# A two-layer block with adaLN: part of the adaLN pieces, and c, loaded by Pool's queue instead of SyncE's

## The chip, the cores and the metric

The kernel runs on one core of one Trainium2 chip. The metric is the time of one execution on the device, in microseconds (us). The core has five engines that work side by side, each through its own instructions in their order: TensorE (PE: matmuls; PEld: its weight loads), VectorE (DVE), ScalarE (ACT), GpSimd (POOL) and SyncE (SP). SP computes nothing here; its queue issues transfers between memory and the chip. ACT's and POOL's queues can issue transfers too. An instruction that waits for a semaphore holds up everything behind it on its own engine. All transfers are carried by the core's 16 DMA engines.

## The reference

Two layers over one sequence of 256 rows of 2048 features, all in float32. A vector c of 2048 numbers gives, by a large matrix per layer, six rows of 2048: shift, scale and gate for the mixer, and the same for the feed-forward (adaLN).

```python
c_act = jax.nn.silu(c)
for i in range(DEPTH):                       # 2 layers
    ada = c_act @ ada_w[i] + ada_b[i]        # ada_w[i]: 2048 x 12288
    shift1, scale1, gate1, shift2, scale2, gate2 = jnp.split(ada[:, None, :], 6, axis=-1)
    h = rms_norm(x, norm1_g[i]) * (1.0 + scale1) + shift1
    m = diff_attention(h, ...) if i == 0 else mamba2_ssd(h, ...)
    x = x + gate1 * m
    h = rms_norm(x, norm2_g[i]) * (1.0 + scale2) + shift2
    x = x + gate2 * swiglu(h, ffn_w_gate_up[i], ffn_w_down[i])   # hidden 5632
```

Layer 0 mixes by differential attention, layer 1 by a Mamba-2 block (SSD): a projection to 4096 gates z, 6144 channels that pass a short convolution, and 64 step sizes; a chunked scan over two chunks of 128 rows; and a projection from 4096 back to 2048.

## The kernel before

**Stages.** The work runs through attention, the first feed-forward, the SSD block and the second feed-forward, one after another. Every weight matrix is read once, in units of 256 rows by 512 columns, 512 KB each. A unit is loaded by SP into one of seven raw buffers (L284, `split_unit`). ACT copies it to its high part `wh` in a reduced format (L288), DVE subtracts to get the low part `wl` (L290; the profile shows every DVE and PE operation under L137, the helper that issues them), and TensorE multiplies twelve times: two row blocks, two k tiles, and the products high by high, low by high, high by low. Up to four units stand ready ahead of TensorE.

**Order.** The order is written by the program itself. Units go through a list; when one is taken out and multiplied, `tick` runs: it gives each open chain of small steps (a Python generator in `active`) one step (`step_all`), and, at a rate set per stage, takes adaLN jobs from the list `jobs`.

**adaLN.** The adaLN products are spread under the other work as pieces of 512 KB, each loaded into one of the same seven raw buffers and consumed by DVE one tick later. There are two kinds. For shift and scale, `col_jobs` (L506) loads 128 output features by half of c's length (L514), and DVE multiplies by c, which stands in all partitions as the two tiles `cB`, and sums along the row (`raw<-raw,cB` in the profile). For a gate, `ada_job` (L461) loads 128 rows of the matrix by 1024 columns (L474; the bias at L472) and DVE adds it, times an entry of c, to the tile `acc` (`acc<-raw,cT,acc`). When a half of 1024 columns is complete, `fin_gate` (L526) has Pool sum `acc` over the 128 partitions, 512 columns at a time, into the gate row (L532), two all-reduces per half.

The stages take the following jobs. At the first feed-forward's entry, `jobs0` (L1469) queues shift and scale of layer 1's mixer and 16 of the pieces for its feed-forward, and stores c to memory (L1478), as the room of `cB` is taken by `acc` later. While its down products run, gate 2 of layer 0 is made (`down`, L1405, 34 pieces). At the SSD block's entry, `later_jobs` (L1491) fetches c again (L1494) and queues the 48 pieces left over, then gate 1 of layer 1 (34 pieces); the rate stays 0 until the scan begins (L1787). The second feed-forward makes its own gate (34 pieces).

**What else is on the queues.** SP also loads the scan's decay tables (L1664), one per group of heads. ACT issues the DMA transposes of the feed-forward's activations (L1372). Pool computes the reciprocal roots of the norms (`rstd_of`, L448 and L449), issues a few small loads and the stores of the output, and fills constants at the SSD block's entry (L1510 to L1513).

Of the kernel before, what the change touches and what calls it, by code (L numbers as in the profile page):

```python
# [35 lines left out]
ADA_UNITS = 156  # L36
# [77 lines left out]
def block_kernel(ctx: ExitStack, tc: tile.TileContext, x, c, positions, norm1_g, norm2_g, ada_w, ada_b,  # L114
# [8 lines left out]
    pe, act, dve, pool, sp = nc.tensor, nc.scalar, nc.vector, nc.gpsimd, nc.sync  # L123
# [47 lines left out]
    def bcast(ap1, n):  # L171
        return bass.AP(tensor=ap1.tensor, offset=ap1.offset, ap=[[0, 128], [1, n]])
# [7 lines left out]
    limit = {"u": W_BUFS}  # L180
    jobs = deque()
    ripe = deque()
    ada = {"rate": 0.0, "acc": 0.0}
    free = {"wk": 3, "po": 1, "epi": EPI, "e0": 3, "e1": 1, "on": 1}

    def take(what, n=1):
# [10 lines left out]
    def start(gen):  # L197
        if next(gen, StopIteration) is not StopIteration:
            active.append(gen)
        return gen  # L200
# [77 lines left out]
    def call(fn):  # L278
        fifo.append(("c", fn))
# [121 lines left out]
    class Columns:  # L401
# [12 lines left out]
        def finish(self, i):  # L414
            t = self.groups[i][0]
            n = t.shape[1]
            ps = bank("wk")
            pe.transpose(ps[:, :n], self.st[:n, i, :], ident[:n, :n])
            dve.tensor_copy(t, ps[:, :n])
# [39 lines left out]
    mods = {}  # L459

    def ada_job(layer, vec, finish, gate=False):  # L461
        st = {}
        last = 16 if gate else 15

        def unit(hf, k):
            def run():
                col = vec * D + hf * 1024
                raw = rawp.tile([128, 2, 512], F32, tag="raw", name="raw")
                rv = raw.rearrange("p a n -> p (a n)")
                load["dma"] += 1270.0  # L470
                if k == 16:
                    sp.dma_start(rv, bcast(ada_b[layer, col:col + 1024], 1024))  # L472
                else:
                    sp.dma_start(rv, ada_w[layer, k * 128:(k + 1) * 128, col:col + 1024])  # L474

                def use():
                    if k == 0:
                        st["acc"] = rowp.tile([128, 1024], F32, tag="acc", name="acc", bufs=2)
                        dve.tensor_scalar(st["acc"], rv, cT[:, 0:1], None, op0=ALU.mult)
                    else:  # L480
                        acc = st["acc"]
                        dve.scalar_tensor_tensor(acc, rv, 1.0 / 128.0 if k == 16 else cT[:, k:k + 1], acc,
                                                 op0=ALU.mult, op1=ALU.add)
                    if k == last:
                        acc = st["acc"]
                        ripe.append([1, lambda: finish(acc, hf)])
                ripe.append([RIPE, use])
            return run
        for hf in range(2):
            for k in range(last + 1):  # L490
                jobs.append(unit(hf, k))

    cB = []

    def col_item(layer, vec, kt, hf):
        at = (((4 * layer + (0, 1, 3, 4).index(vec)) * 16 + kt) * 2 + hf) * 131072
        return bass.AP(tensor=ada_t.tensor, offset=ada_t.offset + at, ap=[[1024, 128], [1, 1024]])

    def col_sum(st, rv, layer, vec, kt, hf, t):

        if hf == 0:
            st[kt] = small(1, "half")
        dve.tensor_tensor_reduce(rv, rv, cB[hf], 1.0, st[kt] if hf else b_cols[layer, vec][:, kt:kt + 1],
                                 ALU.mult, ALU.add, t[:, kt:kt + 1] if hf else st[kt])

    def col_jobs(layer, vec, key, g=None):  # L506
        t = mods["T" if g is None else "S", key] = const.tile([128, 16], F32, name=f"col{vec}{key}")
        st = {}

        def unit(kt, hf):  # L510
            def run():
                rv = rawp.tile([128, 2, 512], F32, tag="raw", name="raw").rearrange("p a n -> p (a n)")
                load["dma"] += 1270.0
                sp.dma_start(rv, col_item(layer, vec, kt, hf))  # L514

                def use():
                    col_sum(st, rv, layer, vec, kt, hf, t)
                    if g is not None and (kt, hf) == (15, 1):
                        dve.scalar_tensor_tensor(t, t, 1.0, g, op0=ALU.add, op1=ALU.mult)
                ripe.append([RIPE, use])  # L520
            return run
        for kt in range(16):
            for hf in range(2):
                jobs.append(unit(kt, hf))

    def fin_gate(key):  # L526
        def f(acc, hf):
            if hf == 0:
                mods["G", key] = rowp.tile([128, D], F32, tag="gate", name="gate")
            for i in range(2):  # L530
                o = hf * 1024 + i * 512
                pool.partition_all_reduce(mods["G", key][:, o:o + 512], acc[:, i * 512:(i + 1) * 512], 128,  # L532
                                          ReduceOp.add)
        return f


# [365 lines left out]
    gate = {"next": 0, "raws": []}  # L902
# [434 lines left out]
    def ffn(layer, end, first_jobs, final):  # L1337
        key = f"f{layer}"
# [5 lines left out]
        def enter():  # L1344
            end["leave"]()
            if layer == 0:
                ssd_consts()
            st["low"] = low.enter_context(tc.tile_pool(name=f"low{layer}", bufs=1))
            st["top"] = top.enter_context(tc.tile_pool(name=f"top{layer}", bufs=1))
            first_jobs()  # L1350
            ada.update(rate=len(jobs) / 164, metered=0)
        aT = []

        def gate_done(bk, sg):
# [91 lines left out]
    def ssd_consts():  # L1446
        const2 = ctx.enter_context(tc.tile_pool(name="const2", bufs=1))
        for nm, n in (("cw0", 96), ("cw1", 96), ("cb", 80), ("dsk", 64), ("aneg", 64), ("dtb", 64)):
            H[nm] = const2.tile([128, n], F32, name=nm)
# [17 lines left out]
    cd = tc.dram_tile([1, 2048], F32, name="cd")  # L1467

    def jobs0():  # L1469
        col_jobs(1, 0, "m1")  # L1470
        col_jobs(1, 1, "m1", n1c[1])
        n = len(jobs)
        col_jobs(1, 3, "f1")
        col_jobs(1, 4, "f1", n2c[1])
        while len(jobs) > n + F1_EARLY:
            later.appendleft(jobs.pop())
        for i in range(2):
            sp.dma_start(cd[0:1, i * 1024:(i + 1) * 1024], cB[i][0:1, :])  # L1478

    end = ffn(0, end, jobs0, False)  # L1480
    if upto == "ffn0":
        dump(end)
# [8 lines left out]
    def later_jobs():  # L1491
        for i in range(2):
            cB[i] = rowp.tile([128, 1024], F32, tag="acc", name="cB", bufs=2)
            sp.dma_start(cB[i], bass.AP(tensor=cd.tensor, offset=cd.offset + i * 1024, ap=[[0, 128], [1, 1024]]))  # L1494
        jobs.extend(later)
        later.clear()

    def enter():
        end["leave"]()
        S["y0"] = ph.enter_context(tc.tile_pool(name="y0", bufs=1))  # L1500
        sd = phd.enter_context(tc.tile_pool(name="sd", bufs=1, side="right"))
        S["cb"] = sd.tile([128, 8, 384], F32, name="cb")
        for nm in ("dt", "acum"):
            S[nm] = sd.tile([128, 2, 64], F32, name=nm)
        for nm in ("toend", "eac1"):
            S[nm] = sd.tile([128, 64], F32, name=nm)
        S["gp"] = phd.enter_context(tc.tile_pool(name="gp", bufs=1, side="right"))
        bp = S["bp"] = phb.enter_context(tc.tile_pool(name="bp", bufs=1, side="right"))
        S["all1"] = bp.tile([128, 128], F32, name="all1")
        pool.memset(S["all1"], 1.0)  # L1510
        tri = S["tri"] = bp.tile([128, 128], F32, name="tri")
        pool.memset(tri, 1.0)
        pool.affine_select(out=tri, in_=tri, pattern=[[1, 128]], compare_op=ALU.is_ge, fill=0.0,  # L1513
                           base=0, channel_multiplier=-1)
        S["bc"] = bp.tile([128, 16, 256], F32, name="bc")
        later_jobs()
        ada_job(1, 2, fin_gate("m1"), gate=True)
        ada.update(rate=0.0)

    def tap(j, ct):  # L1520
# [263 lines left out]
            flush_steps()  # L1784
        hl[cp, g] = split_act([(lambda t, b=b: t[:, :, b * 128:(b + 1) * 128], S["yT", g][:, b]) for b in range(2)])

    call(lambda: ada.update(rate=len(jobs) / ADA_UNITS))  # L1787
    for g in range(8):
        bk = Banks()
        norm.push(wi, 4096 + g * 512, 512, bk, True)  # L1790
# [85 lines left out]
```

## Time and profile before

| | us |
|---|---|
| median of 3 runs | 2662.99 |
| lowest and highest | 2661.54, 2674.63 |
| the profiled execution | 2662.98 |
| its span, first to last instruction | 2661.3 |
| busy: PE, DVE, ACT, POOL | 2604.5, 1879.0, 1396.2, 205.7 |

The mean granted TensorE clock is 0.998 of full speed. In the profile's rows, an operation stands with its line, its engine and what it writes and reads (`out<-in`, buffer numbers left out). A `q` behind an engine's name marks its queue's own instructions. The number behind x is a count; durations are in us or, where a mean is given for one instruction, in ns. Behind an arrow in brackets stands what ended the idle time before an instruction. The stages lie about so: attention to 500 us, the first feed-forward to 1240, the SSD block to 1930, the second feed-forward to the end.

### The profile page before, as it was taken

What the parts mean: (1) busy time and instruction counts of PE and PEld (TensorE: products, weight loads), DVE (VectorE), ACT (ScalarE), POOL (GpSimd) and SP (SyncE); (2) the same over time, 40 slices, a digit from 0 to 9 for tenths busy, and PEclk for the clock granted to TensorE, in tenths of its full rate; (3) what the DMA queues carried; (4) which work ended last, traced back from release to release, by engine and by line L of the source; (5) the groups of instructions that cost most, each with busy time, mean ns of one, the idle gap of its engine ahead of it and who ended that gap; (6) DMA issues with size and microseconds to landing.
All of it is one profiled execution on the core that took longest, in us unless ns stands there. A gap on an engine that the chain in (4) does not pass through costs nothing.

```text
span 2661.3 us, 36421 instructions
## 1 busy us (share of the span) xinstructions
PE 2604.5 (98%) x13536; PEld 2175.2 (82%) x13537; DVE 1879.0 (71%) x2335; ACT 1396.2 (52%) x1919; POOL 205.7 (8%) x282
## 2 busy tenths in 40 slices
PE   7999999999999999999999999999999999999999
PEld 4777777788888887888999889987888888888887
DVE  3779887866667666777778888897654444446776
ACT  5445565644444455556556556564564444445554
POOL 5004331000000000101000000011000000000101
PEclk9999999999999999999999999999999999999999
DMA  9997988699899988785578777777656767666775
GB/s 331 333 340 289 323 303 331 226 301 298 295 274 323 310 271 267 281 295 185 166 251 285 263 278 276 261 262 247 226 156 208 206 204 207 203 208 234 292 285 185
DMA packets 235113, 697.15 MB, mean 262 GB/s; under 512 B 68227, under 2 KB 68564, under 8 KB 233526
## 3 DMA queue, kind: packets, MB, share of 16 engines
q1 hardware_dynamic: 186308, 679.64, 73.3%
q10 hardware_dynamic: 47186, 11.74, 3.9%
q0 software_dynamic: 1440, 3.44, 0.5%
q8 instruction: 106, 1.74, 0.3%
q14 instruction: 73, 0.60, 0.1%
HBM read 681.02 MB, written 2.17 MB: 257 GB/s over the span
## 4 chain that ended last, share of the span: by engine, by line
PE 78%; DMA 8%; DVE 7%; issue 3%; ACT 3%; POOL 1%; SPq 0%; ACTq 0%; DVEq 0%; POOLq 0%
PE mm L137 64%; PE wk L137 11%; PE po L137 4%; DMA raw<-in_da_w_in 3%; DVE wl L137 3%; DMA raw<-in_ffn_w_gate_up 2%; ACT wh L288 1%; DVE raw L137 1%; DMA raw<-in_da_w_out 1%; DMA raw<-in_ada_t 1%; DVE x L137 1%; DMA raw<-in_ffn_w_down 1%; ACT x L1043 0%; DVE mx L137 0%; ACT word L1382 0%
## 5 line engine op out<-in xcount | busy, mean ns | idle before, releaser
L288 ACT CAST wh<-raw 128x1024 fp32r<-128x1024 f32 (+1 forms) x888 | 924.9, 1046 | 1101.4 <-PE mm L137 642.2
L137 DVE TENSOR_TENSOR wl<-raw,wh 128x1024 fp32r<-128x1024 f32 (+1 forms) x888 | 1077.7, 1224 | 511.9 <-ACT wh L288 507.8
L137 PE MATMUL mm<-wh,ah 128*128 128x512 f32 (+1 forms) x2560 | 1011.4, 395 | 7.2 <-ACT wh L288 3.3
L137 PE MATMUL mm<-wl,ah 128*128 128x512 f32 (+1 forms) x2560 | 997.9, 390 | 2.7 <-DVE wl L137 2.7
L137 PE MATMUL mm<-wh,al 128*128 128x512 f32 (+1 forms) x2560 | 997.9, 390 | 0.0
L137 PEld LDWEIGHTS mm<-wh,ah 128*128 128x128 f32 x2560 | 481.2, 188 | 118.2 <-issue 12.1
L137 PEld LDWEIGHTS mm<-wl,ah 128*128 128x128 f32 x2560 | 481.5, 188 | 103.4 <-DVE wl L137 5.7
L137 PEld LDWEIGHTS mm<-wh,al 128*128 128x128 f32 x2560 | 481.0, 188 | 101.4 <-DVE al L137 0.6
L137 PE MATMUL wk<-wl,ah 128*128 128x512 f32 x360 | 140.5, 390 | 5.1 <-DVE wl L137 5.1
L532 POOL PARTITION_ALL_REDUCE gate<-acc x12 | 43.5, 3673 | 1288.1 <-DVE acc L137 1281.3
L137 DVE CUSTOM_DVE_ANT_0 raw<-raw,cB,half 128x1024 f32<-128x1024 f32 x110 | 140.8, 1280 | 0.6 <-DMA raw<-in_ada_t 0.2
L137 DVE CUSTOM_DVE_ANT_0 raw<-raw,cB,bias 128x1024 f32<-128x1024 f32 x110 | 140.7, 1279 | 0.0
L137 PE MATMUL wk<-wh,al 128*128 128x512 f32 x360 | 140.3, 390 | 0.0
L137 PE MATMUL wk<-wh,ah 128*128 128x512 f32 x360 | 140.3, 390 | 0.0
L137 PE MATMUL mm<-ah,wh 128*128 128x256 f32 x720 | 118.8, 285 | 0.0
L137 PE MATMUL mm<-ah,wl 128*128 128x256 f32 x720 | 117.7, 283 | 0.0
L137 PE MATMUL mm<-al,wh 128*128 128x256 f32 x720 | 117.7, 283 | 0.0
L137 DVE SCALAR_TENSOR_TENSOR acc<-raw,cT,acc 128x1024 f32<-128x1024 f32 x90 | 114.9, 1277 | 0.0
L137 PEld LDWEIGHTS mm<-ah,wh 128*128 128x128 f32 x720 | 100.2, 192 | 0.1
L137 PEld LDWEIGHTS mm<-ah,wl 128*128 128x128 f32 x720 | 100.2, 192 | 0.0
L137 PEld LDWEIGHTS mm<-al,wh 128*128 128x128 f32 x720 | 100.2, 192 | 0.0
L137 DVE TENSOR_TENSOR al<-word,ah 128x512 fp32r<-128x512 f32 x44 | 28.5, 688 | 93.3 <-ACT ah L393 93.3
(312 smaller groups left out, 2161.8 us busy)
## 6 DMA issues: line engine op xcount, KB each, us to landing
raw<-in_ffn_w_gate_up SPq DMA_DIRECT2D x352, 512.0 KB, 4.6
raw<-in_ada_t SPq DMA_DIRECT2D x220, 512.0 KB, 5.5
raw<-in_ffn_w_down SPq DMA_DIRECT2D x176, 512.0 KB, 5.6
raw<-in_ssd_w_in SPq DMA_DIRECT2D x136, 512.0 KB, 4.8
raw<-in_da_w_in SPq DMA_DIRECT2D x96, 512.0 KB, 5.9
raw<-in_ada_w SPq DMA_DIRECT2D x96, 512.0 KB, 5.4
raw<-in_ssd_w_out SPq DMA_DIRECT2D x64, 512.0 KB, 4.8
raw<-in_ada_m SPq DMA_DIRECT2D x60, 512.0 KB, 6.0
```

The source lines that it names most:

```text
L137: return fn(dst, *a, **k)
L288: act.copy(wh[:, :, :n], raw)
L532: pool.partition_all_reduce(mods["G", key][:, o:o + 512], acc[:, i * 512:(i + 1) * 512], 128, ReduceOp.add)
```

## The change

The dictionary `ada` gets the entry `queue`, which is SP's at first, Pool's from the first feed-forward's entry on, and SP's again from the second's. The loads at L472, L474 and L514 are issued by it. The store of c and its fetches go to Pool for good. The fetch of c, the 48 left-over jobs and the gate's jobs are written down at the scan's begin instead of at the block's entry. The two all-reduces of a gate's half become a chain of steps: the first at once, the second after three further steps of `step_all`.

```diff
-    ada = {"rate": 0.0, "acc": 0.0}
+    ada = {"rate": 0.0, "acc": 0.0, "queue": sp}
...
-                    sp.dma_start(rv, bcast(ada_b[layer, col:col + 1024], 1024))
+                    ada["queue"].dma_start(rv, bcast(ada_b[layer, col:col + 1024], 1024))
                 else:
-                    sp.dma_start(rv, ada_w[layer, k * 128:(k + 1) * 128, col:col + 1024])
+                    ada["queue"].dma_start(rv, ada_w[layer, k * 128:(k + 1) * 128, col:col + 1024])
...
-                sp.dma_start(rv, col_item(layer, vec, kt, hf))
+                ada["queue"].dma_start(rv, col_item(layer, vec, kt, hf))
...
-            for i in range(2):
-                o = hf * 1024 + i * 512
-                pool.partition_all_reduce(mods["G", key][:, o:o + 512], acc[:, i * 512:(i + 1) * 512], 128,
-                                          ReduceOp.add)
+
+            def steps():
+                for i in range(2):
+                    o = hf * 1024 + i * 512
+                    pool.partition_all_reduce(mods["G", key][:, o:o + 512], acc[:, i * 512:(i + 1) * 512], 128,
+                                              ReduceOp.add)
+                    for _ in range(3):
+                        yield
+            start(steps())
...
-            ada.update(rate=len(jobs) / 164, metered=0)
+            ada.update(rate=len(jobs) / 164, metered=0, queue=sp if layer else pool)
...
-            sp.dma_start(cd[0:1, i * 1024:(i + 1) * 1024], cB[i][0:1, :])
+            pool.dma_start(cd[0:1, i * 1024:(i + 1) * 1024], cB[i][0:1, :])
...
-            sp.dma_start(cB[i], bass.AP(tensor=cd.tensor, offset=cd.offset + i * 1024, ap=[[0, 128], [1, 1024]]))
+            pool.dma_start(cB[i], bass.AP(tensor=cd.tensor, offset=cd.offset + i * 1024, ap=[[0, 128], [1, 1024]]))
...
-        later_jobs()
-        ada_job(1, 2, fin_gate("m1"), gate=True)
         ada.update(rate=0.0)
...
-    call(lambda: ada.update(rate=len(jobs) / ADA_UNITS))
+    def scan_jobs():
+        later_jobs()
+        ada_job(1, 2, fin_gate("m1"), gate=True)
+        ada.update(rate=len(jobs) / ADA_UNITS)
+    call(scan_jobs)
```

## The prediction, made before the changed kernel ran

> **What bounds the kernel now.** I read the page first, then the table of windows over the stretch in which the changed queue is used, then the waits of SP's queue, then single transfers in the timeline.
>
> ```profile
> span 2661.3 us, 36421 instructions
> ...
> PE 2604.5 (98%) x13536; PEld 2175.2 (82%) x13537; DVE 1879.0 (71%) x2335; ACT 1396.2 (52%) x1919; POOL 205.7 (8%) x282
> ```
>
> TensorE is busy for nearly the whole span. That figure alone proves little, because the ends of matmuls are modelled; the windows show where it does stand still. The columns are stretch, length, busy time of each engine with its count, granted clock, busy share of the DMA engines, GB/s.
>
> ```profile
> 550.00:1857.00 1307.00, 1297.49 (x6937) 1119.47 (x6937) 1003.35 (x1227) 704.71 (x911) 57.86 (x51) 1.00 0.81 269
> 550.00:1005.00 455.00, 454.72 (x2008) 376.21 (x2008) 309.82 (x353) 215.77 (x221) 2.16 (x4) 1.00 0.95 293
> 1005.00:1035.00 30.00, 27.48 (x119) 21.91 (x118) 18.32 (x17) 13.64 (x14) 0.00 (x0) 1.00 0.96 253
> 1330.00:1780.00 450.00, 449.01 (x2909) 406.41 (x2908) 392.34 (x521) 268.02 (x406) 28.96 (x30) 1.00 0.76 269
> 1780.00:1857.00 77.00, 73.63 (x321) 60.13 (x320) 62.30 (x64) 36.20 (x50) 9.78 (x6) 0.98 0.72 247
> 1853.00:1857.00 4.00, 4.00 (x13) 3.13 (x12) 2.87 (x3) 0.53 (x2) 0.00 (x0) 0.57 0.81 247
> ```
>
> From 550 to 1857 us, which is the first feed-forward and the SSD block without the crossing into them, TensorE is idle for 1307.00 − 1297.49 = 9.5 us. To that comes one short stretch at a granted clock of 0.57 (1853 to 1857), worth 4.00 × (1 − 0.57) = 1.7 us. So even a change that removed every stall here would gain 9.5 + 1.7 = 11.2 us, and the idle time is mostly in two places: 2.5 us at 1005 to 1035, 3.4 us at 1780 to 1857. In the gate and up products (550 to 1005) TensorE loses 0.3 us, while the DMA engines are busy 0.95 of the time. That is the place to fear, not the place to hope for.
>
> The profiled execution took 2662.98 us, its span 2661.3, so 1.7 us lie around it; the median of the runs is 2662.99. A measurement here can tell about 0.5% from no change, 13.3 us. The bound of 11.2 us is under that.
>
> **What is moved off SP's queue.** The issues from 500 to 1823 us, by tile: count, size, median time to landing.
>
> ```profile
> raw<-in_ada_t SPq DMA_DIRECT2D x128, 512.0 KB, 5.4
> ...
> raw<-in_ada_w SPq DMA_DIRECT2D x64, 512.0 KB, 5.3
> ...
> raw<-in_ada_b SPq DMA_DIRECT2D x4, 512.0 KB, 5.5
> cB<-cd SPq DMA_DIRECT2D x2, 512.0 KB, 7.1
> ```
>
> These are 128 + 64 + 4 = 196 adaLN pieces, the two fetches of c, and two small stores of c that go with them. All pass from SP to Pool. The second feed-forward's 34 pieces stay on SP. What SP waits for in 550 to 1857 (total, times, longest):
>
> ```profile
> SPq L284 <- DVE wl L137: 491.9, 274, 14.5
> SPq L514 <- DVE wl L137: 148.0, 99, 3.5
> SPq L474 <- DVE wl L137: 87.2, 54, 6.5
> ```
>
> SP waits for buffers that VectorE is still reading. It is not short of time to issue; it already runs as far ahead as the seven raw buffers allow. A piece on Pool's queue needs the same buffer and so is issued at the same moment, as long as Pool is free. So removing the pieces from SP gives weights no earlier buffer, except where SP stands for another reason. One such place carries idle time of TensorE, 1005 to 1035, behind the last DMA transposes of the gate and up products, where ScalarE waits for a weight:
>
> ```profile
> ACT wh L288 <- DMA raw<-in_ffn_w_down: 10.3, 3, 8.6
> ```
>
> There, weights stand in SP's queue behind pieces, which will be gone. I cannot read from this trace how much of the 2.5 us goes: its ends are 0 (the transposes alone hold the weights) and 2.5 us. I take half, **−1.3 us**, being nearer to neither. In the scan (1330 to 1780) SP also stands for the decay table's buffer, but TensorE's idle time is 450.00 − 449.01 = 1.0 us; I take 0 of that, with 1.0 as the end.
>
> In a sentence that the sum can do without: the Trainium skill, "DMA: Bandwidth & Descriptors", section "Issuing engines are not separate DMA queues", says that transfers from any engine end on the same 16 DMA engines, and that starting them from several engines saves only the sequencer's issue time. By that rule, as SP's issue time binds nothing here, the result would be 2663.0 in place of my 2661.7.
>
> **What Pool takes on.** Pool's own loads in this trace, six of 256 KB each, and how long an issue holds it (second number, ns):
>
> ```profile
> L1272 POOL DMA_DIRECT2D x<-in_x x6 | 3.4, 568 | 44.8 <-DVE res L137 44.6 <-issue 0.2
> ```
>
> 196 issues × 0.568 us = 111 us on an engine that is busy 57.86 us of these 1307. That is hidden by Pool's idleness. What could cost is order: Pool executes in order, and its queue holds, besides loads, the rstd pairs (L448, L449) and the gates' all-reduces (L532), which wait for data of the present. SP had nothing of that kind, and ran ahead. The worst case in the trace is a piece that SP issues just before an rstd that precedes it in the program:
>
> ```profile
> 1573.22 0.37 SPq L514 DMA_DIRECT2D raw<-in_ada_t  x1
> ```
> ```profile
> 1576.95 1.04 POOL L448 TENSOR_SCALAR yr<-yss 128x1 f32<-128x1 f32 x1 [42.47 <-ACT junk L456]
> 1578.07 0.55 POOL L449 TENSOR_TENSOR yr<-yr,neghalf 128x1 f32<-128x1 f32 x1
> ```
> ```profile
> 1587.36 1.28 DVE L137 CUSTOM_DVE_ANT_0 raw<-raw,cB,half 128x1024 f32<-128x1024 f32 x1
> ```
>
> On Pool it can go only at 1578.62, 5.4 us later than now, and VectorE reads it at 1587.36. It keeps 8.7 us. That equals the shortest interval that any of the 196 has today, which costs VectorE nothing:
>
> ```profile
> 1029.74 0.33 SPq L474 DMA_DIRECT2D raw<-in_ada_w  x1
> ```
> ```profile
> 1038.43 1.28 DVE L137 SCALAR_TENSOR_TENSOR acc<-raw,cT,acc 128x1024 f32<-128x1024 f32 x1
> ```
>
> Against a landing time of 5.4 us both have 3.3 us to spare. Landing from Pool's queue is not in the trace for 512 KB; its six loads of 256 KB (L1272, four of them issued at once) landed so:
>
> ```profile
> DMA to landing us min/median/max: 3.4/7.1/10.0
> ```
>
> At the median, 7.1, nothing is late. At 10.0, such a piece is 10.0 − 8.7 = 1.3 us late, and VectorE with the weights' low parts behind it; perhaps four such places could reach TensorE, 4 × 1.3 = 5 us. I take 0, because the median leaves room, and keep **0 to +5 us**. In the other direction, an rstd behind a piece waits for that piece's buffer; but SP issued every piece that precedes an rstd before that rstd began, so its buffer was free by then, and the delay is the issue's 0.57 us, ahead of a product two steps off. Nothing.
>
> **c at the scan.** Pool meets the two fetches in its queue right after the triangle's mask at the block's entry, with nothing to wait for between; the step at which they are written down doesn't hold them back. First reader of c in the block:
>
> ```profile
> 1250.34 0.29 POOL L1513 TENSOR_SCALAR_AFFINE_SELECT tri<-tri 128x128 f32<-128x128 f32 x1
> ```
> ```profile
> 1346.51 1.28 DVE L137 CUSTOM_DVE_ANT_0 raw<-raw,cB,bias 128x1024 f32<-128x1024 f32 x1
> ```
>
> About 96 us for a landing of 7.1. Cost 0. The jobs queued with them were held at rate 0 until that step already, and their count and rate are the same.
>
> **The gate's two sums.** Now they run back to back:
>
> ```profile
> 1099.28 7.58 POOL L532 PARTITION_ALL_REDUCE gate<-acc  x2 [460.36 <-DVE acc L137]
> ```
>
> Three steps apart is an order in Pool's queue, not a delay: the second sum's data is there, so it only lets the pieces written down between go first. After the first half of a gate there are such pieces; they go one sum, 7.58 / 2 = 3.8 us, earlier than behind both. After the second half there are none, and the two sums run as now. **0 us.**
>
> Sum: 2662.98 − 1.3 + 0 = **2661.7 us**.
>
> **Rivals.**
>
> *A, slower: the DMA engines become the bound in the gate and up products.* There they are busy 0.95 of 455 us; 22.8 us are free. Where Pool's and SP's loads ran side by side, in 438 to 446 us, the packets cost (packets, MB, share of 16 engines):
>
> ```profile
> DMA packets 862, 3.04 MB, mean 380 GB/s; under 512 B 122, under 2 KB 122, under 8 KB 861
> ...
> q1 hardware_dynamic: 541, 1.98, 62.5%
> q0 software_dynamic: 320, 1.05, 39.3%
> ```
>
> Over 8 us that is 2.53 us per MB for SP's queue and 2.99 for Pool's, 0.47 more. The issues of 550 to 1005:
>
> ```profile
> raw<-in_ada_t SPq DMA_DIRECT2D x74, 512.0 KB, 5.4
> ...
> raw<-in_ada_w SPq DMA_DIRECT2D x3, 512.0 KB, 4.5
> ```
>
> These 77 pieces (40.4 MB) would add 18.9 us, which still fits in 22.8. At twice this surcharge it is 37.9, and 15.1 us stand outside: 2662.98 + 15.1 = **2678 us**. The point from which it decides is 0.56 us per MB. For it: the margin is thin and 320 packets are a small sample, with transposes not among them. Against it: the busy share is stretched by waiting, since the same engines carried 380 GB/s there and carry 293 here.
>
> *B, faster: the sums really come apart.* If the second sum of the SSD gate is held until the residual has passed, VectorE is not slowed under it:
>
> ```profile
> 1840.45 2.62 DVE L137 TENSOR_TENSOR x<-x,res 128x512 f32<-128x512 f32 x1
> ...
> 1846.66 0.69 DVE L137 TENSOR_TENSOR x<-x,res 128x512 f32<-128x512 f32 x1
> ```
>
> The same operation takes 2.62 us beside the sum and 0.69 after it. All of the stall at 1780 to 1857 with its low clock would then go, 3.37 + 1.7 = 5.1 us: **2656.6 us**. Against it: nothing stands between the two sums on Pool, and the residual began while the first still ran, so no wait ties them.
>
> *C, nothing moves:* the transposes alone hold the weights at 1005 to 1035, **2663.0 us**.
>
> **How the numbers follow.** The forecast gets 0.70, C 0.12, B 0.08, A 0.10. Only A leaves the band of 13.3 us, and the bound of 11.2 us keeps B and all gains together inside it; I leave 0.03 for a faster result by something not seen here, taken from the forecast: faster 0.03, same 0.87, slower 0.10. Range: below, 2662.98 − 2.5 − 1.0 − 5.1 = 2654.4, all gains and B together; above, no gain, the 5 us of late pieces, and A at one and a half times the surcharge (28.4 − 22.8 = 5.6): 2673.6.
>
> **What would show it.** Right: 196 more issues on Pool of about 0.57 us; landings near 5 to 7 us; VectorE with no wait on a piece over 1 us; TensorE's idle time from 1005 to 1035 smaller, in 550 to 1005 still under 1 us; the sums near 1836 still back to back. Wrong: ScalarE waiting for gate and up weights until TensorE stands (A); a cost per MB on Pool's queue above SP's by over 0.56 us; VectorE standing for pieces behind an rstd; or a time under 2652, which would mean that the pace of the matmuls themselves hung on SP's queue, which nothing above shows.

## The result, and the profile after

| | median (us) | lowest to highest | runs |
|---|---|---|---|
| before | 2664.03 | 2659.19 to 2680.35 | 21 |
| changed | 2685.58 | 2667.63 to 2699.14 | 21 |

The ratio is 1.007, 95% interval 1.0052 to 1.0089: the changed kernel is slower by 14 to 24 us. The forecast was 2661.7 us, its range ended at 2673.6, and the slower side had a chance of 0.10. The forecast was wrong.

The profiled execution of the changed kernel took 2697.11 us, 11.5 more than its median; I read places and shares from it, and the size of the change from the medians. Its page begins:

```profile
span 2695.4 us, 36495 instructions
...
PE 2620.5 (97%) x13537; PEld 2182.3 (81%) x13537; DVE 1879.9 (70%) x2335; ACT 1395.9 (52%) x1919; POOL 312.7 (12%) x482
```

The table of windows of the changed kernel, with the stretches that the prediction used and two more (stretch, length, busy time of PE, PEld, DVE, ACT, POOL, granted clock, DMA share, GB/s):

```profile
550.00:1857.00 1307.00, 1282.97 (x6816) 1102.88 (x6815) 976.90 (x1201) 689.38 (x888) 151.91 (x240) 0.99 0.82 264
550.00:1005.00 455.00, 436.69 (x1867) 355.74 (x1866) 291.31 (x333) 194.45 (x198) 41.16 (x78) 0.97 0.98 279
1330.00:1780.00 450.00, 448.80 (x3023) 411.95 (x3022) 383.89 (x522) 262.95 (x393) 58.20 (x95) 1.00 0.76 266
1055.00:1075.00 20.00, 18.03 (x73) 14.44 (x72) 14.12 (x13) 10.20 (x12) 1.59 (x3) 0.91 0.75 263
1870.00:1895.00 25.00, 21.57 (x87) 17.04 (x86) 20.48 (x21) 12.10 (x20) 7.35 (x2) 0.93 0.60 200
```

Nearly all of the loss lies in the gate and up products. From 550 to 1005 us TensorE was idle for 0.3 us before; now it is idle for 455.00 − 436.69 = 18.3 us, and a mean clock of 0.97 in place of 1.00 costs about 0.03 × 455 = 13.7 us more (the clock has two places, so this can be off by some 2 us). The 18.0 us of new idle time and the 13.7 make 31.7 of the 34.1 us by which this span is longer than the one before. The count of matmuls agrees: 2008 − 1867 = 141 fewer in the same stretch, at 455.00 / 2008 = 0.227 us each 32 us. The scan (1330 to 1780) is as it was. The two stalls of before are still there, only later: the crossing into the down products at 1055 to 1075, the gate's sums with the residual at 1870 to 1895.

Who waited in 550 to 1005 us: first the kernel before, one row, then the changed kernel (total us, times, longest):

```profile
ACT wh L288 <- DMA raw<-in_ffn_w_gate_up: 73.2, 45, 5.7
```
```profile
DVE wl L137 <- ACT wh L288: 162.9, 112, 12.6
ACT wh L288 <- DMA raw<-in_ffn_w_gate_up: 132.1, 58, 12.8
...
PEld mm L137 <- ACT wh L288: 16.4, 6, 4.5
PE mm L137 <- ACT wh L288: 13.9, 6, 4.1
```

ScalarE waits for gate and up weights, up to 12.8 us at a time, and TensorE waits for ScalarE. One such gap in the timeline of TensorE, changed kernel (start, length, operation, idle time before it):

```profile
800.06 0.39 PE L137 MATMUL mm<-wl,ah 128*128 128x512 f32 x1
800.29 0.39 PE L137 MATMUL mm<-wh,al 128*128 128x512 f32 x1
804.79 0.79 PE L137 MATMUL mm<-wh,ah 128*128 128x512 f32 x1 [4.11 <-ACT wh L288]
...
807.07 0.63 PE L137 MATMUL mm<-wh,ah 128*128 128x512 f32 x1
807.50 0.63 PE L137 MATMUL mm<-wl,ah 128*128 128x512 f32 x1
```

Before the gap a matmul starts every 0.23 us, after it every 0.43 us. So a gap costs its length, and then a few us at half pace. The Trainium skill, "TensorE: Matmul & The Clock Gate", section "What's actually happening", says that the clock is halved after an idle window of about 3.4 us; the 4.11 us here agree.

Where do the weights come late? Inside the DMA transposes. DMA queues while one pair of transposes ran, first the kernel before from 783 to 800 us, then the changed kernel from 788 to 818 us (q1 is the queue of SP, q10 that of ScalarE with the transposes, q0 Pool's; packets, MB, share of 16 engines; then issues and median us to landing):

```profile
q1 hardware_dynamic: 883, 3.19, 74.0%
q10 hardware_dynamic: 1817, 0.46, 37.0%
...
raw<-in_ffn_w_gate_up SPq DMA_DIRECT2D x5, 512.0 KB, 13.1
raw<-in_ada_t SPq DMA_DIRECT2D x2, 512.0 KB, 9.9
aT<-halves ACTq DMA_TRANSPOSE x1, 17.8
```
```profile
q1 hardware_dynamic: 710, 2.60, 52.2%
q10 hardware_dynamic: 2053, 0.51, 47.9%
q0 software_dynamic: 379, 1.34, 13.5%
...
raw<-in_ffn_w_gate_up SPq DMA_DIRECT2D x6, 512.0 KB, 14.1
raw<-in_ada_t POOLq DMA_DIRECT2D x4, 512.0 KB, 16.2
```

Beside one pair 3.65 MB passed in 17 us before (transposes included), 215 GB/s; now it is 4.45 MB in 30 us, 148 GB/s. SP's queue falls from 883 / 17 = 52 packets per us to 710 / 30 = 24, the transposes from 107 to 68.

This is the pair with the gap above, and not every pair goes so. Two others of the changed kernel, 744 to 766 and 889 to 915 us:

```profile
q1 hardware_dynamic: 822, 2.97, 49.3%
q0 software_dynamic: 425, 1.55, 36.4%
```
```profile
q1 hardware_dynamic: 859, 3.12, 41.7%
q0 software_dynamic: 433, 1.59, 40.5%
```

With the transposes they move 229 and 201 GB/s; SP's queue has 37 and 33 packets per us. TensorE has no idle time around the first (740 to 775 us) and 4.8 us around the second (885 to 925). Two more pairs, issued from 653 to 703 us, landed in about 6 us at the median, and TensorE had no idle time there. So the third queue doesn't draw out every pair, but where the weights fall far behind, TensorE stands.

One more thing happens beside a pair. ScalarE issues the transposes, and the issue of the second can hold it. The longest issue, before and after (start, length):

```profile
783.81 4.81 ACTq L1372 DMA_TRANSPOSE aT<-halves  x1
```
```profile
789.84 9.68 ACTq L1377 DMA_TRANSPOSE aT<-halves  x1
```

ScalarE also makes `wh`, so a long issue could by itself keep TensorE waiting. At this place the weight came later still: the issue ended at 799.52, and ScalarE could begin only with the weight's landing, at 803.69.

### The profile page after: what moved, and what is told of

It reads as the page before. It is cut to its first block, busy times and chain, and to the rows that moved or that the text cites. A ratio compares the mean times of both kernels' runs of the same rounds, so it can differ in the third digit from the quotient of the medians.

```text
span 2695.4 us, 36495 instructions
## 1 busy us (share of the span) xinstructions
PE 2620.5 (97%) x13537; PEld 2182.3 (81%) x13537; DVE 1879.9 (70%) x2335; ACT 1395.9 (52%) x1919; POOL 312.7 (12%) x482
## 4 chain that ended last, share of the span: by engine, by line
PE 76%; DMA 9%; DVE 7%; ACT 3%; issue 3%; POOL 1%; SPq 0%; ACTq 0%; DVEq 0%; POOLq 0%
PE mm L137 62%; PE wk L137 11%; DMA raw<-in_ffn_w_gate_up 5%; PE po L137 4%; DVE wl L137 3%; ACT wh L288 1%; DMA raw<-in_da_w_in 1%; DMA raw<-in_ada_t 1%; DVE raw L137 1%; DMA raw<-in_da_w_out 1%; DVE x L137 0%; DMA raw<-in_ffn_w_down 0%; ACT x L1048 0%; ACT word L1387 0%; DVE al L137 0%
## 5 line engine op out<-in xcount | busy, mean ns | idle before, releaser
L514 POOL DMA_DIRECT2D raw<-in_ada_t x128 | 68.3, 533 | 693.9 <-DVE wl L137 594.7
```

What stands on the lines that cost most here:

```text
L514: ada["queue"].dma_start(rv, col_item(layer, vec, kt, hf))
```

## The experiments

The theories at the start. T1: the DMA engines serve the queues in turn, and a third queue beside the transposes and the weights takes the weights' share. T2: a byte on Pool's queue costs the engines more (rival A as I priced it). T3: Pool's program order delays pieces or holds buffers. T4: c or the split sums. Each ratio below is against the kernel before on the same chip, from 5 rounds, with its 95% interval.

**Where it is: which of the moved loads.** The queue is chosen at the entry of the feed-forward; each edit is to the changed kernel.

```
 # pieces on Pool from the down products on
-            ada.update(rate=len(jobs) / 164, metered=0, queue=sp if layer else pool)
+            ada.update(rate=len(jobs) / 164, metered=0, queue=sp)
...
             flush_jobs()
+            ada["queue"] = sp if layer else pool
```

> Only the 116 pieces from the down products and the SSD block on go to Pool's queue; the 80 pieces of the gate and up products stay on SP; c and the split sums as in the changed kernel. Theory T1 (turns: the DMA engines serve the queues in turn, and beside the DMA transposes a third queue takes the weights' share): the loss lies in the gate and up products alone, so 0 +- 4 us against before. T2 (a byte on Pool's queue costs the DMA engines more, wherever they are nearly full): also near 0, at most +5 us, because they are fullest in the gate and up products. T3 (Pool's program order: pieces wait behind Pool's other work, or hold raw buffers out of turn): the loss goes with the number of pieces, 116/196 of 21 us = +12 us. T4 (c or the split sums): the whole +21 us.

Measured: 2664.77 us against 2660.07, ratio 1.0015 (0.9996 to 1.0033).

```
 # pieces on Pool in the gate and up products only
             flush_jobs()
+            ada["queue"] = sp
```

> The complement: the 80 pieces of the gate and up products on Pool's queue, the 116 later ones back on SP; c and the split sums as in the changed kernel. T1 and T2: the whole loss, +21 us (between +15 and +30), with TensorE's gaps in 600 to 1000 us only. T3: 80/196 of 21 us = +9 us. T4: +21 us.

Measured: 2686.99 against 2660.07, ratio 1.008 (1.0053 to 1.0107). Its window from 550 to 1005 us:

```profile
550.00:1005.00 455.00, 436.81 (x1886) 356.47 (x1885) 292.18 (x334) 196.62 (x201) 40.63 (x77) 0.98 0.99 282
```

It is the same picture as the changed kernel: 18.2 us idle and a lower clock.

```
 # no piece on Pool; c and the split sums as in the changed kernel
-            ada.update(rate=len(jobs) / 164, metered=0, queue=sp if layer else pool)
+            ada.update(rate=len(jobs) / 164, metered=0, queue=sp)
```

> No piece on Pool's queue at all; only c by Pool at the scan and the split sums. T1, T2, T3: 0 +- 4 us against before. T4: +21 us.

Measured: 2660.12 against 2660.07, ratio 0.9997 (0.9985 to 1.001). T4 falls, and so does T3, which wanted +12 us for the 116 later pieces: their interval ends at +8.8. The 80 pieces of the gate and up products carry the loss.

**Is it the transposes.** In both kernels the first feed-forward's 22 DMA transposes are left out:

```
-                    act.dma_start_transpose(t[:, :, b * 128:(b + 1) * 128], halves)
+                    if layer:
+                        act.dma_start_transpose(t[:, :, b * 128:(b + 1) * 128], halves)
+                    else:
+                        act.copy(t[:, :, b * 128:(b + 1) * 128], halves.rearrange("p (k t) -> p k t", k=8))
```

> The kernel before, with the 22 DMA transposes of the first feed-forward left out and ScalarE copying the halves in their place, untransposed: the values after it are not those of the reference. All queues as before. Every theory: about the time before, 0 to -6 us, since TensorE already loses under 5 us in the gate and up products and the 2.5 us behind the last transposes may go. It is the partner of the next run.

> The changed kernel with the same 22 transposes left out (values after it differ from the reference's). If the loss needs the DMA transposes (T1 in any form: what a further filled queue does beside them): equal to its partner, 0 +- 4 us. If bytes on Pool's queue, or its order, cost by themselves (T2, T3): +10 to +21 us over the partner.

Measured: 2656.1 for the kernel before without them, ratio 0.9976 (0.9962 to 0.999); 2657.63 for the changed one, ratio 0.9987 (0.9977 to 0.9997). The rows of 550 to 1005 us, first of the kernel before without transposes, then of the changed one without them:

```profile
550.00:1005.00 455.00, 455.00 (x2011) 376.72 (x2010) 312.51 (x352) 237.14 (x243) 2.15 (x4) 1.00 0.84 282
```
```profile
550.00:1005.00 455.00, 455.00 (x2011) 376.71 (x2009) 312.18 (x352) 235.70 (x241) 42.73 (x81) 1.00 0.82 281
```

The two intervals overlap, and the pair lies 0.0011 apart, 2.9 us. Without transposes 40 MB on Pool's queue cost next to nothing, and TensorE never stands. The harm needs both.

**Is it Pool's queue, or one queue more.** Two edits of the kernel before. In the first every second weight of the gate and up products goes on Pool's queue and the pieces stay on SP; in the second weights and pieces all go on Pool's queue, so that SP's is empty.

```
 # weights alternate (SP and Pool), in split_unit
+        ada["turn"] = ada.get("turn", 0) + 1
+        q = pool if ada.get("both") and ada["turn"] % 2 else sp
-        sp.dma_start(raw.rearrange("p a n -> p (a n)")[:, :2 * n], w.unit(row, col, n))
+        q.dma_start(raw.rearrange("p a n -> p (a n)")[:, :2 * n], w.unit(row, col, n))
```

> The kernel before, its pieces and c on SP as they were, but every second weight of the first feed-forward's gate and up products on Pool's queue: 85 loads or so, 44 MB, somewhat more than the 40 MB of pieces that the change puts there. Here too three queues are in use beside the transposes, but the weights hold two of them. T1: the weights' share beside the transposes doesn't fall, 0 +- 5 us against before, and a pair of transposes may last longer. T2: 44/40 of 21 us = +23 us, since the bytes on Pool's queue are more. If any third queue does the harm, however filled: +21 us.

Measured: 2682.85 against 2660.07, ratio 1.007 (1.005 to 1.009).

```
 # all on Pool, in split_unit and in col_jobs; the queue is Pool's in the gate and up products only
-        sp.dma_start(raw.rearrange("p a n -> p (a n)")[:, :2 * n], w.unit(row, col, n))
+        ada["queue"].dma_start(raw.rearrange("p a n -> p (a n)")[:, :2 * n], w.unit(row, col, n))
...
-                sp.dma_start(rv, col_item(layer, vec, kt, hf))
+                ada["queue"].dma_start(rv, col_item(layer, vec, kt, hf))
```

> The kernel before with pieces and weights of the gate and up products all on Pool's queue, in their old order: SP's queue is empty, so two queues are in use beside each other as before, Pool's and the transposes'. If a third filled queue does the harm: 0 +- 6 us against before, and transposes as short as before. If bytes on Pool's queue cost the DMA engines more (T2): 126 MB in place of 40, far above the changed kernel's +21 us, +40 us or more.

Measured: 2660.21 against 2660.41, ratio 0.9997 (0.9982 to 1.0011). The queues of that kernel from 550 to 1005 us, and its window:

```profile
q0 software_dynamic: 33742, 122.50, 78.9%
q10 hardware_dynamic: 23288, 5.78, 9.9%
q1 hardware_dynamic: 1304, 4.75, 3.3%
```
```profile
550.00:1005.00 455.00, 455.00 (x2010) 376.76 (x2010) 311.21 (x352) 216.79 (x221) 125.11 (x236) 1.00 0.93 293
```

T2 falls: three times the bytes on Pool's queue, 122.50 MB, and no loss. But T1 missed as well: with the weights on two queues I expected no loss, and there was as much as before. The queues of the alternating kernel during one pair of transposes, 741 to 768 us:

```profile
q1 hardware_dynamic: 749, 2.74, 50.9%
q10 hardware_dynamic: 2009, 0.50, 32.2%
q0 software_dynamic: 372, 1.34, 25.2%
...
raw<-in_ffn_w_gate_up POOLq DMA_DIRECT2D x3, 512.0 KB, 17.6
raw<-in_ffn_w_gate_up SPq DMA_DIRECT2D x3, 512.0 KB, 11.5
```

SP's and Pool's queues together carry 4.08 MB in 27 us, 151 GB/s; before it was 3.19 MB in 17 us on one queue, 188 GB/s. In another pair of this kernel, 834 to 858 us, it was 188. The second bulk queue doesn't add to the first. And Pool's gets half as much as SP's: since TensorE uses the weights in order, every second one at 1.34 MB in 27 us would set the pace of all; that this is the reason is argued, not shown. So T1 has to be put otherwise: not whose loads stand on the third queue matters, but that bulk loads are split over two queues while the transposes run on a third.

**Where on the way.** Some pieces of the gate and up products on Pool, the others on SP: first those written down 10 or more weight units after a pair's halves are ready, then those of the units 0 to 5.

```
+        ada["since"] = ada.get("since", 99) + 1
+        if ada.get("gate_up"):
+            ada["queue"] = pool if ada["since"] >= 10 else sp      # the other run: 0 <= ada["since"] < 6
...
+            ada["since"] = -1
             active.append(by_dma())
```

> The changed kernel with only those pieces of the gate and up products on Pool's queue that are written down 10 or more weight units after a pair of transposes (32 of 80); the other 48, which lie beside a pair, and all from the down products on, on SP. If the loss comes from Pool's queue being filled while transposes run: 0 to +6 us against before (a few issues still reach into a burst). If it goes with the bytes on Pool's queue: 32/80 of 21 us = +8 us or more.

> The partner of the run with 32 pieces away from the transposes: of the gate and up products' pieces, the 29 that are written down 0 to 5 weight units after a pair's halves are ready go on Pool's queue, so beside the transposes; everything else on SP. If only what is on Pool's queue while transposes run does harm, most of the loss is back: +14 to +21 us, although it is fewer bytes than in the partner. If the harm goes with the bytes on Pool's queue, wherever: 29/80 of 24 us = +9 us.

Measured: away, 2667.92 against 2660.41, ratio 1.0023 (1.0006 to 1.0041); near, 2672.26 against 2661.37, ratio 1.0024 (1.0002 to 1.0047). So about +6 us each; the medians are 7.5 and 10.9 us apart. That is what the number of pieces gives (+8 and +9), not what the place gives. In the units I chose, the two are no clean test of the place: a transfer lands up to 20 us after its issue, and the transposes of both kernels are met by some of Pool's pieces. The pair shows that the loss grows with what is on the third queue, and leaves the place open.

**Which queue the transposes are on.** The first feed-forward's transposes are issued by SP, in the kernel before and in the changed one:

```
-                    act.dma_start_transpose(t[:, :, b * 128:(b + 1) * 128], halves)
+                    (act if layer else sp).dma_start_transpose(t[:, :, b * 128:(b + 1) * 128], halves)
```

> The kernel before, with the first feed-forward's 22 DMA transposes issued by SP in place of ScalarE: one queue carries weights, pieces and transposes. If the transposes drag on because they share the engines with another queue: bursts of a few us, -2 to -5 us against before. What can go against it: SP waits for a pair's halves, with weights behind it in its queue, some us each; if that outweighs, +5 us or more. It is also the measure of that wait for the next run.

> The changed kernel with the same transposes on SP: two queues are in use in the gate and up products, SP's with weights and transposes, Pool's with the pieces. If three filled queues at once do the harm: as its partner with the transposes on SP, 0 +- 5 us between them. If it is bulk loads split over two queues beside transposes, however these are issued: +15 to +21 us over the partner.

Measured: 2658.42 against 2662.65 for the kernel before with transposes on SP, ratio 0.9987 (0.9975 to 0.9999); 2664.04 for the changed kernel with them on SP, ratio 1.0002 (0.9987 to 1.0017). All pieces are on Pool's queue in the second, as in the changed kernel, and against the kernel before nothing measurable is left of the loss of 0.7%. Between the partners lie 0.0015, 4 us by the ratios (their intervals overlap) and 5.6 by the medians: about the edge of what three queues at once predicts (0 ± 5), and far from +15 to +21. The trace of the second has 455.00 − 452.17 = 2.8 us of idle time of TensorE in the stage, where its partner has none, so a few us of loss may be left. How long a transpose takes to land from 550 to 1005 us, in five fences: the kernel before, the changed one, all on Pool, before with transposes on SP, changed with transposes on SP:

```profile
aT<-halves ACTq DMA_TRANSPOSE x22, 9.2
```
```profile
aT<-halves ACTq DMA_TRANSPOSE x20, 14.0
```
```profile
aT<-halves ACTq DMA_TRANSPOSE x22, 7.8
```
```profile
aT<-halves SPq DMA_TRANSPOSE x22, 3.1
```
```profile
aT<-halves SPq DMA_TRANSPOSE x21, 3.7
```

In line with the weights they land in 3 to 4 us. And the engines have time again; the window of the kernel before with transposes on SP shows a DMA share of 0.82 at 290 GB/s, where it was 0.95 at 293:

```profile
550.00:1005.00 455.00, 455.00 (x2011) 376.71 (x2010) 308.00 (x352) 214.39 (x220) 2.15 (x4) 1.00 0.82 290
```

**A version that might have beaten both.** The kernel before, with the pieces held back beside the transposes:

```
+        ada["since"] = ada.get("since", 99) + 1
+        if ada.get("gate_up"):
+            ada["rate"] = 0.0 if 2 <= ada["since"] < 10 else ada["gate_up"]
...
+            ada["gate_up"] = 0.0 if layer else len(jobs) / 84
```

> A version that might beat both: the kernel before, all on SP, with the gate and up products' pieces held back for the weight units 2 to 9 after a pair's halves are ready, and issued at 80/84 a unit outside them. If the transposes drag on because SP's queue is full of pieces and weights beside them: bursts of 3 us in place of 20, and -2 to -6 us against before (not more: without any transposes it was -6). If it is the weights alone that drag them: 0 +- 2 us. If the denser pieces outside starve the weights there (200 + 190 GB/s wanted): +5 us or more.

Measured: 2661.35 against 2661.37, ratio 0.9994 (0.9977 to 1.0011): no gain. The transposes landed no sooner, and ScalarE waited oftener but never long (this kernel, 550 to 1005 us, one row of the DMA issues, one of the waits):

```profile
aT<-halves ACTq DMA_TRANSPOSE x21, 18.1
```
```profile
ACT wh L291 <- DMA raw<-in_ffn_w_gate_up: 171.0, 98, 6.1
```

The holding back failed: three pieces still lie beside the pair of 784 to 806 us in this kernel, so it doesn't tell whether it is pieces or weights that draw the transposes out.

```profile
raw<-in_ada_t SPq DMA_DIRECT2D x3, 512.0 KB, 14.1
```

What it does show is that long transposes by themselves cost little: they take 18.1 us to land here, 14.0 in the changed kernel, and TensorE is idle for 3.4 us in the stage (455.00 − 451.58) in place of 18.3. Long issues on ScalarE alone don't make the loss either: 8 of the 22 took over 4 us here, up to 7.37, and 2 of 22 in the changed kernel. The longest single wait of ScalarE for a weight doesn't order the runs: 6.1 us here and 12.8 in the changed kernel, but 7.7 in the run with only the 80 pieces on Pool's queue, which lost as much, and 9.4 in the one with only the 116 later pieces, where TensorE was idle for 3.9 us. The version that does beat both is the one above with weights, pieces and transposes all on SP's queue, by 0.13% of the kernel before (0.01 to 0.25%), so by little.

## Why the prediction was wrong

**The step that failed.** "A piece on Pool's queue needs the same buffer and so is issued at the same moment, as long as Pool is free. So removing the pieces from SP gives weights no earlier buffer, except where SP stands for another reason." The part on buffers held as far as the waits show: in the gate and up products SP stood 315 us for VectorE before (weights and pieces) and 310 after. I stopped there: the sum has terms for issue, buffers and the pieces' landing, and none for what the pieces, on a queue of their own, do to the landing of the weights. I took that as 0. It measured 21.6 us by the medians, 2685.58 − 2664.03.

How it comes about can be worked out from the rows, as an estimate. Before, 155 weights of 0.524 MB went out in 455 us, so they need 179 GB/s. Beside a pair of transposes in the kernel before they get 5/7 of 3.19 MB in 17 us, 134 GB/s: over those 17 us they fall 0.8 MB behind, 1.5 loads, which the buffers ahead cover. In the changed kernel they get 2.60 MB in 30 us, 87 GB/s, and fall 2.8 MB behind, over five loads; there are four weight buffers, and TensorE stood at 800 us. The other pairs fit this: at 744 to 766 us weights get 135 GB/s and fall under two loads behind, without idle time; at 889 to 915 us they get 120 GB/s and fall nearly three behind, with 4.8 us. The order of need is lost too: in one queue a weight waits only for the pieces needed before it, in two it shares with pieces that aren't needed yet. A late landing also holds back later issues: SP's waits that end with the landing of a weight grew from 6.4 us to 80.9. How much each part has, the runs don't tell.

**Rival A** had the place, the sign and nearly the size (2678), by a mechanism that is refuted: no surcharge per MB on Pool's queue shows with 122.50 MB on it. So its size was luck. My price came from 438 to 446 us, where no transposes ran; the prediction says so, and gave that little weight. The range, too, ended at 2673.6, below this rival's own time, although it had a chance of 0.10. Against A I argued that the busy share of 0.95 is stretched by waiting. That was right, the same bytes take 0.82 with the transposes on SP; the error was to read room out of it, since the stretch stays as long as transposes have a queue to themselves.

**The gain of 1.3 us at 1005 to 1035** didn't come. The stall stands at 1055 to 1075 in the changed kernel (20.00 − 18.03 = 2.0 us idle). With only the later 116 pieces off SP's queue, those that stood there between the weights of the down products, no gain was measured either (1.0015; the interval's lower end is 0.9996, −1.1 us). And the stall isn't in every execution: in the trace with no piece on Pool's queue TensorE is busy for all of 1000 to 1100 us, although every piece stood on SP's queue as before. So the term was read from one execution.

**Pool's load and order** held. An issue took 0.53 us, POOL's 41.16 us in the gate and up products are hidden, and the 116 pieces among Pool's own work (rstd, all-reduces) cost 0.0015 (−0.0004 to 0.0033), within the 0 to +5 us that I kept, or somewhat over:

```profile
L514 POOL DMA_DIRECT2D raw<-in_ada_t x128 | 68.3, 533 | 693.9 <-DVE wl L137 594.7 <-DMA raw<-in_ffn_w_gate_up 33.8 <-DVE col4f L137 13.3
```

**Landings** were 6.5 us at the median in the gate and up products, inside the 5 to 7 I gave, and the median misled: it is the landings during a transpose that decide, and those were 14.1 us for weights and 16.2 for pieces from 788 to 818 us.

**c and the sums**: 0 forecast, 0.9997 measured. Rival B is refuted in this trace: the sums still run back to back (one row, 7.35 us for both, in the timeline of the changed kernel), and the stall beside them stays, 25.00 − 21.57 = 3.4 us.

```profile
1870.43 7.35 POOL L534 PARTITION_ALL_REDUCE gate<-acc  x2 [12.52 <-DVE acc L137]
```

**The rule of the Trainium skill** cited in the prediction says that several queues save only issue time, and no run here gains by putting loads on a further queue. Read as "no change" it gave 2663.0, and the measurement decides against that reading: moving loads to another queue cost 0.7%. Another sentence of the same page, the Trainium skill, "DMA: Bandwidth & Descriptors", section "Queues, rings and completion order", bears on it more: each engine goes round between the queues that have work, a packet at a time. The fall of SP's queue from 52 packets per us to between 24 and 37 with a third queue filled agrees in direction; how unequally SP's and Pool's queues were served (749 packets and 372) it doesn't give.

**What stays open.** Why copies and transposes in different queues carry so little together (215 GB/s beside a pair before, 148 to 229 beside three pairs of the changed kernel), when the same transposes in line with the copies cost the engines nothing that can be seen, is not explained by these runs, nor why some pairs drag on and others don't. Leaving the transposes out, or giving them to SP, also frees ScalarE from issuing them, so those runs don't part the late weights from the longer issues; only the run with the pieces held back speaks against the issues alone. A third queue other than Pool's was not tried.

## What to carry to other kernels

Before moving loads to an idle engine's queue, ask what else the DMA engines carry at that time, and price the landing of the urgent loads, not only the issue and the bytes: one queue keeps them in the order of need. Here a stage with TensorE almost never idle and a DMA share of 0.95 had nothing to gain from a further queue, and lost. Where DMA transposes run beside a stream of loads, try them in that stream's own queue; here that was worth 0.13%.

## What the runs showed of the hardware

A DMA transpose of 256 KB lands in 3.1 us when it follows the loads in SP's queue and in 9.2 when it runs beside them from ScalarE's; the engines' busy share for the same bytes is 0.82 and 0.95. Pool's queue alone carries 122.50 MB in 455 us without loss; in one pair beside a filled SP queue and transposes it got 372 packets where SP's got 749. The issue of a transpose can hold ScalarE: mostly 1.25 us, but up to 4.81 before and 9.68 in the changed kernel.
